# A wider opening, joined squares, a new task order and a later place for one gate in a two-layer decoder kernel

## The chip, the cores and the metric

The kernel runs on one core of a Trainium2 chip. Five engines of that core work side by side: TensorE (matmuls; the profile calls its matmuls PE and its weight loads PEld), VectorE (DVE), ScalarE (ACT), GpSimd (POOL) and SyncE (SP, which here only issues transfers). The metric is the device time of one execution in microseconds, as the median of several runs.

## The reference

Two layers run one after the other on 256 tokens of width 1024. Each layer has a token-mixing half and a retrieval half, and both are modulated by six vectors that come from the conditioning `c`:

```python
mod = (c_act @ w_ada + b_ada)[:, None, :]
sh1, sc1, g1, sh2, sc2, g2 = jnp.split(mod, 6, axis=-1)
h = rms_norm(x, norm1_g) * (1 + sc1) + sh1
proj = h @ w_in
q, k, v, cb, cc, ch, su, sv = jnp.split(proj, split_pts, axis=-1)
...
x = x + g1 * (merged @ w_out)
h2 = rms_norm(x, norm2_g) * (1 + sc2) + sh2
x = x + g2 * peer_ffn(h2, peer_wq, peer_sub_keys, peer_down, peer_up)
```

`merged` joins windowed attention with 8 query heads, a short gated convolution and a spatial gate over 128-token chunks, each with a norm of its own. `peer_ffn` projects `h2` to queries, scores them against two sets of 128 keys for each of 8 heads, picks 16 of 128 x 128 experts for each head, and adds their gated outputs. Note where the six vectors are used: `sh1`, `sc1` at the start of a layer, `g1` after the output projection, `sh2`, `sc2` right behind that, and `g2` only when the experts of the layer are done.

## The kernel before

**Layout.** The residual stream `X` lies in on-chip memory with the 1024 features as 8 chunks of 128 partitions and the 256 tokens along the free axis. A large buffer, `arena`, is cut by hand into regions whose use changes from stage to stage.

**Weights.** All weights come in as chunks of 128 x 1024 numbers (512 KB) from one list, `seq` (L352 to L377). `cast_step` takes the next entry of that list. A "mat" entry is split into a high half on ScalarE (L312, L314) and a low half on VectorE (L305, L307), both issued with raised priority (L310), and is used in three cheaper products (L401 to L403). A "whole" entry is used as it is, in one full-precision product (L399). Raw chunks lie in a ring of five buffers of two chunks each; a new transfer waits until both chunks of the oldest buffer have been used. `next_chunk` hands the next weight chunk to TensorE and keeps two more prepared.

**Modulation ("ada" entries).** The six vectors need 48 chunks of `w_ada` for each layer. VectorE multiplies each chunk by the activated `c` and sums along its free axis (L252), so one such entry costs a transfer of 512 KB and one VectorE pass, and no TensorE work. In layer 0 all 48 are spread among the other weights: groups sc1 and sh1 in the opening, g1, sh2 and sc2 among the input projection's chunks, g2 among the first six chunks of the output projection (`mix(tail[:6], ada(0, [5]))`, L363). `mix(a, b, first, last)` puts the entries of b evenly behind those of a between two positions.

**The opening of layer 0** (`first_norm` L454, `first_chunks` L555). The sum of squares is taken over 8 feature chunks: ScalarE squares each chunk (L457), TensorE sums each over its partitions by products with a column of ones (L440). Then follow the root, the reciprocal and a product that spreads the result over all partitions (L424). After that each of 8 row blocks d is taken in turn: two ada entries, a row block of the first `FIRST` input-projection chunks (`w_first[d]`, 128 x FIRST * 128 numbers, into `R_FIRST`), the scaled and shifted chunk d of the input (L450 on VectorE, L452 on ScalarE), and `FIRST` products with it (L559), accumulated in FIRST/2 PSUM banks. `FIRST` is 6, so two query pairs and the key/value pair are done in the opening.

**The rest of the input projection** (`mixing` L588). Chunks `FIRST` to 15 follow, one by one (`chunk`), each pair emptied by ScalarE (`evac`). Behind chunk n the tasks that `PLAN0` lists for n are issued: head sums (`qk_sums`), logits (`lg..`), softmax (`sm..`), transposes (`pt..`), value products (`pv..`), norms and so on. Numbers 16 to 23 stand between the chunks of the output projection. In this part the instructions' order on each engine is found by a list scheduler that follows program order as priority.

**The retrieval half** (`retrieval` L878). A hand-ordered bridge (`bridge` L468) computes the second norm beside the first query chunks; then chunks 4 to 15 of the query projection follow in pairs, with one group of score products for each pair (L995), while VectorE works off top-16 searches (L883 to L891) from a list of filling work. Then 128 expert chunks downwards (L399) and 128 upwards (L1214) run on TensorE, in a hand-written order. Picks become one-hot factors by three transposes for each half of the tokens (L977).

Of the kernel before, what the change touches and what calls it, by code (L numbers as in the profile page):

```python
# [13 lines left out]
AF = mybir.ActivationFunctionType  # L14
# [6 lines left out]
DC = 8  # L21
# [15 lines left out]
WHOLE_PQ = (0, 1)  # L37
WHOLE_OUT = ((4, 5), ())
OUT_ORDER = ((4, 5, 1, 0, 2, 6, 7, 3), (4, 5, 0, 3, 2, 1, 6, 7))
PLAN0 = ((5, 'qk_sums'), (7, 'k_norm lg01'), (8, 'exp sm01'), (9, 'v_tok lg00 sm00'), (10, 'lg10 lg11'), (11, 'pt01 pt00 cz'), (12, 'sm11 inv0 sm10 sg'), (13, 'pt10 pt11 pv0 inv1 ao0'), (14, 'cy as0 gs4 pv1 an0'), (15, 'gn4 mix'), (16, 'ao1 as1 sqrt'), (18, 'an1'), (19, 'gs6'), (20, 'gn6'))  # L40
PLAN1 = ((5, 'qk_sums k_norm'), (6, 'v_tok'), (7, 'lg10 exp'), (8, 'lg01 lg00 sm00'), (10, 'lg11'), (11, 'sm01 cz'), (12, 'sg'), (13, 'pt00 pt01 sm10 pv0'), (14, 'inv0 ao0 cy pt10'), (15, 'sm11 pt11 inv1 gs4 pv1 as0 ao1 gn4 mix'), (16, 'as1 an0'), (17, 'an1 sqrt'), (20, 'gs6 gn6'))
G_LAST = 124
OUT_AT = (3, 5, 6, 7)
# [21 lines left out]
FOLD_LAG = 4  # L65
FILL = 1.5
FILL_DOWN = (2.2, 2.1)
FIRST = 6
SUMS_AT = 5


# [12 lines left out]
def hybrid_trunk(ctx: ExitStack, tc: tile.TileContext, x_in, c_in, vec_in, w_ada, w_first, w_in, w_out, w_pq,  # L84
                 keys, down, down_rows, up, up_rows, rel_bias, sgu_w, sgu_b, out):
    nc = tc.nc
# [57 lines left out]
    X = region(56 * S, DC, S)  # L144
# [12 lines left out]
    R_YS = region(37 * S, DC, S)  # L157
# [45 lines left out]
    class Src:  # L203
# [6 lines left out]
        seq = []  # L210
# [125 lines left out]
    def ada(layer, groups, kind="ada"):  # L336
        return [(kind, w_ada[layer, p], (layer, p)) for g in groups for p in range(8 * g, 8 * g + 8)]
# [15 lines left out]
    for layer in range(DEPTH):  # L353
        body = [("whole" if n in WHOLE_IN[layer] else "mat", w_in[layer, n], None) for n in range(16)]
        tail = [("whole" if k in WHOLE_OUT[layer] else "mat", w_out[layer, k], vec[:, layer, V_OG + k:V_OG + k + 1])
                for k in OUT_ORDER[layer]]
        if layer == 0:
            first = []
            for d in range(DC):
                first += [("ada", w_ada[0, o + d], (0, o + d)) for o in (SC1, SH1)]  # L360
                first.append(("first", w_first[d], R_FIRST[:, d, :]))
            body = first + mix(body[FIRST:], ada(0, [2, 3, 4]))
        body += mix(tail[:6], ada(0, [5])) + tail[6:] if layer == 0 else tail  # L363
        seq += body + [("whole" if n in WHOLE_PQ else "mat", w_pq[layer, n], None) for n in range(16)]
        dn, un = ([("pair", None, None) if n % 2 else ("second" if n % 4 == 0 else "whole", w[layer, n // 2], None)
                   for n in range(128)] for w in (down, up))
        for n, at in enumerate(AHEAD_AT):
            c = AHEAD_FIRST + n
            dn[c] = ("early", down[layer, c // 2, :, c % 2, :], region(at * S, D))
        aside = ada(1, [0, 1, 2, 3, 4] if layer + 1 < DEPTH else [5], "aside")  # L370
        for n, at in reversed(tuple(enumerate(ASIDES_AT[layer]))):
            dn.insert(at, aside[n])
        if layer + 1 < DEPTH:
            un = mix(un, aside[len(ASIDES_AT[layer]):], *ASIDES_UP)
        Src.starts.append(len(seq))
        seq += dn + un
# [76 lines left out]

    def first_norm():  # L454
        ss = bank("g", 2)
        for d in range(DC):
            nc.scalar.activation(R_YS[:, d, :], X[:, d, :], AF.Square)  # L457
            sums(ss, d, d == DC - 1)
        rs = inv_rms(ss)

        def step(d):
            for _ in range(3):
                cast_step()
            scaled(R_HF[:, d, :], mods[0], SC1, SH1, rs, d)

        return step
# [1016 lines left out]
```

## Time and profile before

| | us |
|---|---|
| median of 3 runs | 1558.25 |
| lowest and highest run | 1555.5, 1559.74 |
| the profiled execution, whole time | 1555.62 |
| its span from first to last instruction | 1553.9 |
| opening, until the last product of the row blocks ends | 41.17 |
| first product of the output projection starts | 100.38 |
| first product of the bridge starts | 127.99 |
| score groups of the query projection, first and last | 148.53 to 186.90 |

The page gives busy time of each engine, busy tenths in 40 slices of the span, the transfer queues, and the chain of work that ended last, followed back from the last instruction. Views of the trace give the same for a chosen stretch. In a row of a group, "x32" counts instructions, then come busy time, the mean duration in ns, and the idle time before with what ended it. In a row of the timeline stand start, duration, engine, line, operation, result and operands; the bracket says how long the engine idled before it and what released it. One full-precision product appears as two records.

### The profile page before, as it was taken

What the parts mean: (1) busy time and instruction counts of PE and PEld (TensorE: products, weight loads), DVE (VectorE), ACT (ScalarE), POOL (GpSimd) and SP (SyncE); (2) the same over time, 40 slices, a digit from 0 to 9 for tenths busy, and PEclk for the clock granted to TensorE, in tenths of its full rate; (3) what the DMA queues carried; (4) which work ended last, traced back from release to release, by engine and by line L of the source; (5) the groups of instructions that cost most, each with busy time, mean ns of one, the idle gap of its engine ahead of it and who ended that gap; (6) DMA issues with size and microseconds to landing.
All of it is one profiled execution on the core that took longest, in us unless ns stands there. A gap on an engine that the chain in (4) does not pass through costs nothing.

```text
span 1553.9 us, 28477 instructions
## 1 busy us (share of the span) xinstructions
PE 1532.3 (99%) x11244; PEld 1494.4 (96%) x11244; DVE 1001.7 (64%) x2248; ACT 475.1 (31%) x1357; POOL 502.0 (32%) x424
## 2 busy tenths in 40 slices
PE   8999999999999999999999999999999999999998
PEld 7879999999999999999999899999999999999998
DVE  7787897577787454434457578976777764444434
ACT  2356312465564000000026663133666620000000
POOL 0000125333343434333400001244454445444441
PEclk9999999999999999999999999999999999999999
DMA  9998289999999999999975473899999999999996
GB/s 382 392 371 319 97 318 355 421 421 422 422 420 408 420 423 421 423 423 423 423 279 169 169 258 108 328 360 422 421 424 420 420 422 423 423 423 423 424 423 246
DMA packets 122119, 570.64 MB, mean 367 GB/s; under 512 B 14292, under 2 KB 14820, under 8 KB 89986
## 3 DMA queue, kind: packets, MB, share of 16 engines
q1 hardware_dynamic: 48818, 240.54, 39.1%
q0 software_dynamic: 55744, 202.36, 32.6%
q10 hardware_dynamic: 17424, 125.93, 19.6%
q8 instruction: 88, 1.44, 0.3%
q14 instruction: 45, 0.37, 0.1%
HBM read 563.50 MB, written 4.09 MB: 365 GB/s over the span
## 4 chain that ended last, share of the span: by engine, by line
PE 78%; DMA 8%; issue 6%; DVE 4%; POOL 3%; ACT 1%; SPq 0%; ACTq 0%; POOLq 0%; DVEq 0%
PE acc L1214 37%; PE ch L399 24%; DMA arena<-in_down_rows,arena 6%; PE ch L401 2%; PE ch L402 2%; PE ch L403 2%; POOL arena L1117 2%; DMA raw<-in_w_ada 2%; PE g L1176 1%; PE ch L490 1%; PE g L995 1%; PE acc L401 1%; DVE raw L252 1%; PE acc L403 1%; PE acc L402 1%
## 5 line engine op out<-in xcount | busy, mean ns | idle before, releaser
L1214 PE MATMUL acc<-arena,raw 128*128 128x168 f32 (+1 forms) x4096 | 572.7, 303 | 1.6 <-issue 1.6
L1214 PEld LDWEIGHTS acc<-arena,raw 128*128 128x128 f32 x4096 | 570.4, 190 | 2.4 <-issue 2.4
L399 PE MATMUL ch<-arena,raw 128*128 128x168 f32 (+2 forms) x3808 | 564.4, 307 | 1.9 <-issue 1.9
L399 PEld LDWEIGHTS ch<-arena,raw 128*128 128x128 f32 x3808 | 539.5, 190 | 8.7 <-issue 5.1
L1142 DVE SCALAR_TENSOR_TENSOR spots<-arena,spots 128x1024 f32<-128x1024 f32 x156 | 200.4, 1284 | 237.0 <-DMA arena<-in_up_rows,arena 236.3
L1117 POOL DMA_INDIRECT arena<-in_up_rows,arena x159 | 213.4, 1342 | 289.3 <-DMA arena<-in_up_rows,arena 198.0
L1117 POOL DMA_INDIRECT arena<-in_down_rows,arena x151 | 183.6, 1216 | 227.5 <-DVE arena L1127 167.9
L1127 DVE SCALAR_TENSOR_TENSOR arena<-arena,spots 128x1024 f32<-128x1024 f32 x151 | 183.0, 1223 | 65.6 <-DMA arena<-in_down_rows,arena 61.1
L1160 ACT ACTIVATE arena<-arena,parts 128x128 f16<-128x128 f16 x164 | 64.6, 394 | 128.6 <-DVE arena L1150 114.3
L430 ACT ACT_TABLE_LOAD x6 | 7.7, 1283 | 271.5 <-PE acc L1214 271.4
L401 PE MATMUL ch<-hh,hi 128*128 128x256 f32 x288 | 82.6, 288 | 2.0 <-DVE arena L521 1.9
L402 PE MATMUL ch<-hh,lo 128*128 128x256 f32 x288 | 81.8, 284 | 0.0
L403 PE MATMUL ch<-hh,hi 128*128 128x256 f32 x288 | 81.8, 284 | 0.0
L1193 ACT ACTIVATE arena<-ch 128x336 f32<-128x336 f32 (+32 forms) x122 | 42.2, 346 | 128.1 <-PE ch L399 103.3
L252 DVE SCALAR_TENSOR_TENSOR aside<-aside,arena 128x1024 f32<-128x1024 f32 x48 | 58.6, 1220 | 25.4 <-DMA aside<-in_w_ada 25.4
L252 DVE SCALAR_TENSOR_TENSOR raw<-raw,arena 128x1024 f32<-128x1024 f32 x48 | 58.7, 1228 | 13.2 <-DMA raw<-in_w_ada 9.2
L305 DVE TENSOR_TENSOR lo<-raw,hi 128x1024 fp32r<-128x1024 f32 x42 | 51.2, 1224 | 22.1 <-ACT hi L312 19.2
L399 PE MATMUL ch<-arena 128*128 128x168 f32 (+1 forms) x448 | 63.7, 303 | 1.7 <-issue 1.7
L1186 DVE SCALAR_TENSOR_TENSOR arena<-arena,g 128x336 f32<-128x336 f32 (+30 forms) x82 | 40.4, 492 | 37.9 <-ACT arena L1184 37.0
L399 PEld LDWEIGHTS ch<-arena 128*128 128x128 f32 x448 | 62.6, 190 | 2.2 <-issue 2.2
L1162 ACT ACTIVATE arena<-arena,parts 128x128 f16<-128x128 f16 x164 | 63.4, 386 | 0.0
L1164 ACT ACTIVATE arena<-arena,parts 128x128 f16<-128x128 f16 x164 | 63.4, 386 | 0.0
(237 smaller groups left out, 1722.7 us busy)
## 6 DMA issues: line engine op xcount, KB each, us to landing
raw<-in_up SPq DMA_DIRECT2D x64, 1024.0 KB
raw<-in_up ACTq DMA_DIRECT2D x64, 1024.0 KB
raw<-in_down SPq DMA_DIRECT2D x58, 1024.0 KB
raw<-in_down ACTq DMA_DIRECT2D x56, 1024.0 KB
raw<-in_w_ada SPq DMA_DIRECT2D x48, 512.0 KB
aside<-in_w_ada SPq DMA_DIRECT2D x48, 512.0 KB
raw<-in_w_pq SPq DMA_DIRECT2D x32, 512.0 KB
arena<-in_down SPq DMA_DIRECT2D x28, 512.0 KB
```

The costliest lines, as they stand in the source:

```text
L252: nc.vector.scalar_tensor_tensor(raw, raw, 1.0, cact, op0=OP.mult, op1=OP.mult, accum_out=mods[layer][:, col:col + 1])
L399: nc.tensor.matmul(dst, hi[:, cols], k[0], start=start, stop=stop, **kw)
L401: nc.tensor.matmul(dst, hi[:, cols], k[0], start=start, stop=False, **kw)
L402: nc.tensor.matmul(dst, lo[:, cols], k[0], start=False, stop=False, **kw)
L403: nc.tensor.matmul(dst, hi[:, cols], k[1], start=False, stop=stop, **kw)
L1117: nc.gpsimd.indirect_dma_start(out=held[n], out_offset=None, in_=rows if n >= TS else down_rows[:, :], in_offset=bass.IndirectOffsetOnAxis ...
L1127: nc.vector.scalar_tensor_tensor(row, row, 1.0, R_DX[which(k)[0]], op0=OP.mult, op1=OP.mult, accum_out=R_DOTS[:, k:k + 1])
L1142: nc.vector.scalar_tensor_tensor(R_SUM[s], row, w, R_SUM[s], op0=OP.mult, op1=OP.add)
L1160: nc.scalar.activation(og[0][:, 0, i, :], oh[:, 0, i, :], AF.Copy, scale=parts[:, 0, t + i:t + i + 1])
L1162: nc.scalar.activation(og[1][:, 0, i, :], oh[:, 0, i, :], AF.Copy, scale=parts[:, 1, t + i:t + i + 1])
L1164: nc.scalar.activation(og[0][:, 1, i, :], oh[:, 1, i, :], AF.Copy, scale=parts[:, 0, t + 2 + i:t + 3 + i])
L1214: nc.tensor.matmul(acc[d // 2][:, (d % 2) * S:(d % 2) * S + T], u[:, d * P:(d + 1) * P], acts[:, i, :], start=i == 0 and d % 2 == 0, stop= ...
```

## The change

It has five parts. Constants: `FIRST` is 8 instead of 6, so the opening computes eight chunks with four PSUM banks, `w_first` and `R_FIRST` grow by a third, and the chunks 6 and 7 are no longer in the ring. `PLAN0` gives the tasks of layer 0 another order. In `first_norm` each half of `X` (four feature chunks) is squared by one ScalarE instruction, VectorE adds the second pair of its squares to the first, and TensorE sums two joined chunks instead of four. The eight ada entries of g2 in layer 0 leave the output projection and stand behind chunks 6 to 13 of the query projection (`G2_AT`). Layer 1 has the code that it had.

```diff
-PLAN0 = ((5, 'qk_sums'), (7, 'k_norm lg01'), (8, 'exp sm01'), (9, 'v_tok lg00 sm00'), (10, 'lg10 lg11'), (11, 'pt01 pt00 cz'), (12, 'sm11 inv0 sm10 sg'), (13, 'pt10 pt11 pv0 inv1 ao0'), (14, 'cy as0 gs4 pv1 an0'), (15, 'gn4 mix'), (16, 'ao1 as1 sqrt'), (18, 'an1'), (19, 'gs6'), (20, 'gn6'))
+PLAN0 = ((7, 'qk_sums'), (8, 'k_norm'), (9, 'lg01 exp'), (10, 'sm01 v_tok lg00'), (11, 'sm00 lg10 lg11 cz'), (12, 'pt01 pt00 sm11 sg'), (13, 'inv0 sm10 pt10 pt11 pv0 inv1 ao0'), (14, 'cy as0 gs4 pv1 an0'), (15, 'gn4 mix'), (16, 'ao1 as1 sqrt'), (18, 'an1'), (19, 'gs6'), (20, 'gn6'))
...
-FIRST = 6
+FIRST = 8
+G2_AT = (5, 14)
...
-        body += mix(tail[:6], ada(0, [5])) + tail[6:] if layer == 0 else tail
-        seq += body + [("whole" if n in WHOLE_PQ else "mat", w_pq[layer, n], None) for n in range(16)]
+        queries = [("whole" if n in WHOLE_PQ else "mat", w_pq[layer, n], None) for n in range(16)]
+        seq += body + tail + (mix(queries, ada(0, [5]), *G2_AT) if layer == 0 else queries)
...
         ss = bank("g", 2)
-        for d in range(DC):
-            nc.scalar.activation(R_YS[:, d, :], X[:, d, :], AF.Square)
-            sums(ss, d, d == DC - 1)
+        for half in range(2):
+            at = 4 * half
+            nc.scalar.activation(R_YS[:, at:at + 4, :], X[:, at:at + 4, :], AF.Square)
+            nc.vector.tensor_add(R_YS[:, at:at + 2, :], R_YS[:, at:at + 2, :], R_YS[:, at + 2:at + 4, :])
+            for d in (at, at + 1):
+                sums(ss, d, d == 5)
```

## The prediction

> **What bounds the kernel now.** I read the page first: engines, slices, then the chain of work that ended last.
>
> ```profile
> PE 1532.3 (99%) x11244; PEld 1494.4 (96%) x11244; DVE 1001.7 (64%) x2248; ACT 475.1 (31%) x1357; POOL 502.0 (32%) x424
> PE   8999999999999999999999999999999999999998
> PE 78%; DMA 8%; issue 6%; DVE 4%; POOL 3%; ACT 1%; SPq 0%; ACTq 0%; POOLq 0%; DVEq 0%
> ```
>
> TensorE is busy from slice 2 to the end and carries the chain. So an edit is worth what it does to the time at which TensorE gets through the edited stages; what other engines save counts only where TensorE waits for them. Next, the table by stage (columns: stretch, its length, busy time of PE, PEld, DVE, ACT, POOL, clock, DMA share, GB/s): opening, input projection with attention, output projection, query projection.
>
> ```profile
> 0.00:41.00 41.00, 36.01 (x136) 29.13 (x137) 29.55 (x74) 12.43 (x27) 4.46 (x12) 1.00 0.97 384
> 41.00:100.00 59.00, 58.08 (x317) 47.03 (x315) 47.16 (x112) 25.89 (x72) 1.19 (x2) 1.00 0.98 384
> 100.00:128.00 28.00, 27.07 (x199) 26.16 (x200) 22.62 (x38) 11.54 (x19) 0.00 (x0) 1.00 0.95 372
> 150.00:185.00 35.00, 35.00 (x297) 35.00 (x296) 30.67 (x153) 14.60 (x21) 3.81 (x5) 1.00 0.29 103
> ```
>
> From 41 us on TensorE idles about 1 us in 59 and 1 us in 28, and the transfers run at 0.95 to 0.98 of their capacity up to 128 us. Only the query projection has transfers to spare (0.29). Both limits matter before 128 us, so I follow the chain through the opening.
>
> ```profile
> 13.57 9.06 DMA raw<-in_w_ada
> 22.70 8.86 DMA raw<-in_w_ada
> 31.58 1.24 DVE raw L252 x2
> ...
> 37.75 0.52 ACT arena L452
> 38.31 1.99 PE ch L559 x8
> 40.30 0.86 PE acc L559 x4
> 41.17 0.34 PE g L618 x4
> ```
>
> The opening is set by transfers, then by the last row block: chunk row on VectorE, bias on ScalarE, twelve matmul records (two per product) that end at 41.17. Behind it TensorE runs without a wait.
>
> **Part 1, joined squares.** The rows of the first norm, in time order:
>
> ```profile
> 6.16 6.99 PE L440 MATMUL g<-ones,arena 128*128 128x1 f32 x32
> 7.57 1.33 ACT L457 ACTIVATE arena<-arena 128x256 f32<-128x256 f32 x4 [0.59 <-DMA arena<-in_x_t]
> 8.95 1.22 DVE L252 SCALAR_TENSOR_TENSOR raw<-raw,arena 128x1024 f32<-128x1024 f32 x1 [4.00 <-ACT arena L457]
> 13.18 0.26 ACT L417 ACTIVATE rn<-g,eps 128x2 f32<-128x2 f32 x1 [2.98 <-PE g L440]
> 16.34 3.78 PE L559 MATMUL ch<-arena 128*128 128x256 f32 x8 [1.11 <-ACT arena L452]
> 154.30 1.05 ACT L312 CAST hi<-raw 128x1024 fp32r<-128x1024 f32 x1 [1.63 <-PE ch L403]
> 73.89 0.70 DVE L767 TENSOR_TENSOR arena<-arena 128x512 f32<-128x512 f32 x1
> ```
>
> Removed: six ScalarE squares and 16 of 32 sum records (6.99/32 = 0.218 us each, 3.5 us). Added: two VectorE adds. A square of 1024 columns is not in the trace; the nearest row of that width is 1.05 us, against 1.33 for the four it replaces (bounds 1.0 and 1.33). The add is 0.70. The second half now runs 7.57 + 1.05 + 0.70 + 8 x 0.218 = 11.1 us instead of 13.15, so the norm is about 2.1 us earlier and the first product starts near 14.2 instead of 16.34. If the second add queues behind the first ada chunk (8.95 to 10.17), only 0.9 us is left of that, because the sums wait behind it.
>
> **Part 2, eight chunks in the opening.** Sizes and the slow first products:
>
> ```profile
> raw<-in_w_ada SPq DMA_DIRECT2D x24, 512.0 KB
> arena<-in_w_first SPq DMA_DIRECT2D x8, 384.0 KB
> 19.91 1.91 PE L559 MATMUL acc<-arena 128*128 128x256 f32 x4
> 21.20 2.12 PEld L559 LDWEIGHTS ch<-arena 128*128 128x128 f32 x8
> 54.42 3.46 PE ch L399 x16
> ```
>
> Each row block grows from 384 to 512 KB. Seven of them lie before the last block's data: 7 x 131 KB = 0.92 MB, 2.2 us at about 420 GB/s. The last block starts at 38.31 + 2.2 = 40.5 and now has 16 records, 3.46 us (a whole chunk's row): end 44.0. TensorE's own path: the first 12 records took 16.34 to 21.20, 4.9 us, at half speed; after them 116 records at 3.46/16 = 0.216 make 25.1; 14.2 + 4.9 + 25.1 = 44.2 (45.4 if the second add is late). The two paths meet, so the joined squares are what keeps TensorE from setting the end. I take 44.1, which is 2.9 us later than 41.17. In return two chunks, 2 x 3.46 = 6.9 us, no longer run after it. Net gain 4.0 us, between 2.8 and 4.3.
>
> **Part 3, the projection behind it and the new task order.** Eight chunks are mixed with 24 ada chunks, three to one, instead of ten at 2.4 to one. Total bytes to the end of the stage are unchanged; they are only in another order.
>
> ```profile
> 48.46 1.66 DVE L252 SCALAR_TENSOR_TENSOR raw<-raw,arena 128x1024 f32<-128x1024 f32 x1 [4.56 <-DMA raw<-in_w_ada]
> arena<-in_rel_bias POOLq DMA_DIRECT2D x1, 1024.0 KB
> L252 DVE SCALAR_TENSOR_TENSOR raw<-raw,arena 128x1024 f32<-128x1024 f32 x24 | 29.6, 1236 | 5.8 <-DMA raw<-in_w_ada 5.8
> ```
>
> VectorE waits 4.56 us for a chunk while the bias table comes in on POOL's queue, so arrival sets the pace there. Afterwards one chunk and three ada chunks are 2 MB, 5.0 us per chunk, against 3.46 us of products plus tasks. By that pace the ninth chunk lands near 41, the tenth near 49 (the tables come between), then one each 5 us. TensorE ends the ninth at 47.6 and the head sums near 49.6, and has the key norm and first logits to fill the next gaps. I charge 0.6 us of new idle time (bounds 0, when tasks fill everything, and 2.5, half a chunk's pace, when the tasks wait on VectorE). The tasks are the same instructions in another order, and the fourth PSUM bank of the opening is emptied by ScalarE beside the ninth chunk's products, so neither adds a term.
>
> **Part 4, the last gate moves.** Eight ada chunks leave the output projection. There TensorE idles 0.93 us (28.00 - 27.07), so it can win 0 to 0.9; I take 0.3. They join the query projection, one behind each of chunks 6 to 13, with 512 KB each on SyncE's queue, where the 103 GB/s leave room. Rows that bound the cost:
>
> ```profile
> 156.73 1.21 DVE L305 TENSOR_TENSOR lo<-raw,hi 128x1024 fp32r<-128x1024 f32 x1
> 175.71 1.21 DVE L305 TENSOR_TENSOR lo<-raw,hi 128x1024 fp32r<-128x1024 f32 x1
> 157.14 0.89 PE g L995 x8
> 163.78 0.89 PE g L995 x8
> 177.08 0.89 PE g L995 x8
> 210.84 0.29 DVE L967 TENSOR_TENSOR arena<-arena 128x128 f32<-128x128 f32 x1
> 218.01 0.39 PEld L977 LDWEIGHTS g<-ident,arena 128*128 128x128 f32 x3
> ```
>
> Eight at 1.22 us are 9.8 us of VectorE; it has 35.00 - 30.67 = 4.3 us idle there, so it falls about 5.5 us behind. What TensorE needs of it is only the low half of each chunk. Between two score groups (157.14, 163.78) lie two chunks of (6.64 - 0.89)/2 = 2.9 us; the low half made by 157.9 is used from 160.9, the one made by 176.8 from 180.9: leads of 3 to 4 us. The low halves carry a raised priority, an ada chunk doesn't, so an ada chunk can delay one by at most its own 1.22 us. What falls behind is top-16 work. Its first product for TensorE is ready at 211.1 and used at 218.0: 6.9 us of cover for 5.5. I cost the move at 0; without the cover it is 5.5 to 9.8 us. Two queues see the move as well. On SyncE's the loads behind an ada chunk wait until its buffer pair is free; there are five pairs, so a load is asked for about three chunks (9 us) before its use, and 5.5 us of lag fit in. On ScalarE's own queue one expert load (L287) waits for such a pair with the casts behind it; it is issued four ring items late, about two chunks, which is more than the lag too.
>
> **Sum.** -4.0 + 0.6 - 0.3 + 0 = -3.7 us. Against the profiled execution (1555.62 us; span 1553.9) that is 1551.9. The median of the runs is 1558.25, 2.6 us above that execution; I forecast on the median: **1554.5 us**. About 0.3% (4.7 us) is what a measurement of this kernel can tell from no change, so the likeliest outcome is within it.
>
> **Rivals.**
> 1. *The idle time closes.* The two stages after the opening show 0.92 + 0.93 = 1.85 us of idle TensorE. If the new order and the relieved VectorE remove it, no new idle comes, and Part 2 gives its 4.3: 6.15 us, 1552.1. For it: the idle sits at the seam of attention and output projection, where VectorE was busy 22.62 of 28 us. Against: a wait there can be a dependence (norm, reciprocal, spread) rather than load.
> 2. *Arrival paces the projection.* DMA share 0.98 over 41 to 100 us: if TensorE waits for chunks 9 to 12, and VectorE's ada work delays the softmax, the 4.0 us are spent again: 1557.5 to 1558.5. Against: TensorE's work left in that stage, 58.08 - 6.9 = 51 us, is longer than the 40 us of eight arrivals.
> 3. *VectorE sets the query projection (slower).* If the order of VectorE's queue puts ada and top-16 work ahead of the low halves, TensorE loses 5.5 to 9.8 us between 150 and 185 us and the net is +1.8 to +6.1: 1560 to 1564.4. It decides once VectorE's lag passes the 3 to 4 us lead. For it: 5.5 exceeds the lead. Against: the raised priority.
> [...]
>
> **How the numbers follow.** Forecast 0.44; rival 1 0.20; rival 2 0.18; rival 3 0.13; rival 4 0.05. The runs shown before spread by 4.2 us (1555.5 to 1559.74), so a median may lie 2 us off. The range runs from rival 1 less that, rounded down, 1549.5, to the near end of rival 3, 1560; outside are most of rival 3 (0.12) and the tails of scatter, not over 0.08. Faster by over 0.3% needs more than 4.7 us: rival 1 (0.20), rival 4 without the stall (0.03), and the part of the forecast's own spread beyond 4.7 us (0.07): 0.30. Slower by over 0.3%: rival 3's upper part, 0.10. The rest, 0.60, is within.
>
> **What would show it.** Sums of the first norm at 16 records, ended near 11; the last opening product near 44 and the first output-projection product near 97 instead of 100.4; the first bridge product near 124 instead of 128; in the query projection score groups still 6.6 us apart and PE at 35 of 35; the first pick transposes without a wait before them. I am wrong if the opening ends past 45.5, if chunks of the projection wait on transfers for over 2 us in sum, or if the score groups spread.

## The result: slower by half a per cent, and where the time went

The changed kernel took 1567.63 us in the median of 11 runs (1563.1 to 1576.2), the kernel before 1560.79 us in 11 runs (1555.5 to 1562.8). The medians differ by 6.8 us; the ratio is 1.0051 with a 95% interval of 1.0036 to 1.0065, some 8 us. The forecast was 1554.5 and the range ended at 1560, so both missed, and the time moved the other way. The profiled execution of the changed kernel took 1566.4 us, its span is 1564.6. One trace below, that of the run sc2_in_output_old_order_g2_later, is of an execution of 1784.86 us at a clock of 0.832 and is not used.

First the page of the changed kernel: engines, PE slices and clock slices.

```profile
PE 1536.1 (98%) x11228; PEld 1497.2 (96%) x11228; DVE 1001.5 (64%) x2250; ACT 478.1 (31%) x1353; POOL 508.3 (32%) x424
PE   8989999999999999999999999999999999999998
PEclk9989999999999999999999999999999999999999
```

The third slice (78 to 117 us) is the only one early on in which PE and PEclk have both lost. The same stretches as in the prediction without the opening, for the changed kernel:

```profile
41.00:100.00 59.00, 53.99 (x280) 43.63 (x278) 45.75 (x108) 29.57 (x74) 3.04 (x5) 0.97 0.97 379
100.00:128.00 28.00, 26.43 (x178) 24.48 (x179) 14.13 (x24) 8.76 (x14) 0.00 (x0) 0.88 0.55 189
150.00:185.00 35.00, 34.83 (x294) 34.83 (x295) 33.33 (x124) 19.36 (x27) 2.62 (x3) 1.00 0.75 280
```

Between 41 and 100 us TensorE now idles 5.0 us where it idled 0.92, and its clock is no longer 1.00. The opening did about what it was charged for:

```profile
7.45 1.87 PE L441 MATMUL g<-ones,arena 128*128 128x1 f32 x8 [1.32 <-DVE arena L460]
10.05 1.87 PE L441 MATMUL g<-ones,arena 128*128 128x1 f32 x8 [0.74 <-DVE arena L460]
14.93 3.52 PE L563 MATMUL ch<-arena 128*128 128x256 f32 x8 [1.17 <-ACT arena L453]
42.93 1.89 PE L563 MATMUL acc<-arena 128*128 128x256 f32 x8
```

The sums have 16 records and end at 11.9, the second add (9.31) stood behind the first ada pass, and the last opening product ends at 44.82, 3.65 us later than 41.17. In return two chunks, 6.92 us, are gone from what follows. But the first output-projection product came at 105.21 instead of 100.38. So about 8.1 us (4.83 + 6.92 - 3.65) were lost between those two points. What TensorE waited for (engine, line, releaser, us, times, longest), first in the kernel before from 40 to 130 us, then in the changed kernel from 41 to 110 us:

```profile
PE g L424 <- DVE rg L418: 1.4, 2, 0.9
PE acc L399 <- DVE arena L718: 0.4, 1, 0.4
```

```profile
PE acc L679 <- ACT arena L669: 3.7, 2, 2.4
PE g L728 <- DVE ra L419: 1.4, 1, 1.4
PE g L425 <- DVE rg L419: 0.9, 1, 0.9
```

Not one wait is for a transfer. The transposes (L679) wait for the exponentials (L669), 3.7 us in all; two norms wait for their reciprocals (L419), 2.3 us. The timeline shows what is behind the longest wait of each kind:

```profile
83.59 1.19 DVE L253 SCALAR_TENSOR_TENSOR raw<-raw,arena 128x1024 f32<-128x1024 f32 x1
84.71 0.88 DVE L776 SCALAR_TENSOR_TENSOR arena<-arena,vec 128x256 f32<-128x256 f32 x2
85.50 0.16 DVE L666 TENSOR_SCALAR m<-m 128x4 f32<-128x4 f32 x1
85.70 0.51 ACT L669 ACTIVATE arena<-arena,m 128x256 f32<-128x256 f32 x1 [2.13 <-DVE m L666]
86.35 1.18 PE L679 MATMUL acc<-ident,arena 128*128 128x128 f32 x4 [2.39 <-ACT arena L669]
87.33 4.80 PE L400 MATMUL ch<-arena,raw 128*128 128x256 f32 x16
...
99.03 1.28 DVE L308 SCALAR_TENSOR_TENSOR lo<-raw,vec,hi 128x1024 fp32r<-128x1024 f32 x1 [0.36 <-ACT hi L315]
100.23 0.16 DVE L419 RECIPROCAL ra<-ra 128x1 f32<-128x1 f32 x1
```

VectorE works through an ada pass (L253) and a convolution step; only then comes the tiny softmax step (L666, 0.16 us), then ScalarE, then TensorE. And the chunk behind it takes 4.80 us, where a chunk of the kernel before takes 3.62 in the same view. The second kind is another: at 99.03 VectorE makes a low half of an output-projection chunk (L308), and the norm's reciprocal stands behind it. Windows of 1 us in the changed kernel (the last three columns are clock, DMA share, GB/s) say why the chunk is slow:

```profile
85.00:86.00 1.00, 0.00 (x0) 0.00 (x0) 1.00 (x7) 0.30 (x1) 0.00 (x0) 1.00 1.04 426
87.00:88.00 1.00, 1.00 (x5) 0.91 (x5) 1.00 (x2) 1.00 (x6) 0.00 (x0) 0.50 1.03 410
...
101.00:102.00 1.00, 0.24 (x2) 0.00 (x0) 1.00 (x2) 0.89 (x1) 0.00 (x0) 0.50 0.95 352
```

The clock is at half (0.50) from about 86.3 to 89.7, behind a gap of 2.4 us, and from about 100 to 106.8 us, where gaps of 1.4 and 0.9 us lie (99.05 and 101.24); a gap of 1.3 us at 75.85 left it at 1.00. Between opening and output projection idle time grew from 1.30 to 6.36 us, by about 5; the other 3 of the 8.1 are put down to the work at half clock there, some 7 us of it (an estimate: at 0.50 that work would lose up to 3.5 us). The sums of the engines by 10 us, first the kernel before, then the changed one, show that the load on VectorE is not new:

```profile
70.00:80.00 10.00, 9.94 (x54) 8.40 (x53) 10.00 (x29) 7.42 (x31) 0.00 (x0) 1.00 1.02 400
80.00:90.00 10.00, 10.00 (x55) 7.31 (x54) 9.27 (x28) 9.20 (x23) 0.00 (x0) 1.00 1.03 418
```

```profile
70.00:80.00 10.00, 8.49 (x41) 6.83 (x40) 10.00 (x26) 5.83 (x22) 0.00 (x0) 1.00 0.98 350
80.00:90.00 10.00, 7.44 (x29) 5.29 (x29) 10.00 (x33) 6.34 (x22) 0.00 (x0) 0.83 1.03 417
```

VectorE was full, or nearly so, in both. Before, TensorE was full as well, and the two hid each other. The change took 6.9 us from TensorE alone.

Further on: the output projection itself neither won nor lost much (first product to first update 25.49 us before, 25.90 after), and about 1.3 us were lost in the bridge (below), so that the score groups of the query projection are 6.6 us late. The rest up to 10.7 us of span comes and goes in the experts and in layer 1, whose code is the same.

### The profile page after: what moved, and what is told of

Read it like the earlier page. It is cut to its first block, busy times and chain, and to the rows that moved or that the text cites. A ratio compares the mean times of both kernels' runs of the same rounds, so it can differ in the third digit from the quotient of the medians.

```text
span 1564.6 us, 28450 instructions
## 1 busy us (share of the span) xinstructions
PE 1536.1 (98%) x11228; PEld 1497.2 (96%) x11228; DVE 1001.5 (64%) x2250; ACT 478.1 (31%) x1353; POOL 508.3 (32%) x424
## 3 DMA queue, kind: packets, MB, share of 16 engines
q0 software_dynamic: 55744, 202.36, 32.4%
## 4 chain that ended last, share of the span: by engine, by line
PE 72%; DMA 15%; DVE 5%; issue 4%; ACT 2%; POOL 2%; SPq 0%; ACTq 0%; DVEq 0%; POOLq 0%
PE acc L1218 36%; PE ch L400 20%; DMA arena<-in_down_rows,arena 10%; DMA raw<-in_w_ada 3%; PE ch L402 2%; PE ch L403 2%; PE ch L404 2%; POOL arena L1121 2%; PE g L1180 1%; DVE raw L253 1%; DMA raw<-in_down 1%; PE g L999 1%; PE ch L494 1%; DVE arena L1131 1%; PE acc L402 1%
## 5 line engine op out<-in xcount | busy, mean ns | idle before, releaser
L1121 POOL DMA_INDIRECT arena<-in_up_rows,arena x159 | 216.6, 1363 | 286.4 <-DMA arena<-in_up_rows,arena 212.3
L1164 ACT ACTIVATE arena<-arena,parts 128x128 f16<-128x128 f16 x164 | 64.6, 394 | 126.8 <-DVE arena L1154 126.8
L253 DVE SCALAR_TENSOR_TENSOR raw<-raw,arena 128x1024 f32<-128x1024 f32 x48 | 58.5, 1224 | 13.4 <-DMA raw<-in_w_ada 12.5
L253 DVE SCALAR_TENSOR_TENSOR aside<-aside,arena 128x1024 f32<-128x1024 f32 x48 | 58.5, 1219 | 7.6 <-DMA aside<-in_w_ada 7.6
L1166 ACT ACTIVATE arena<-arena,parts 128x128 f16<-128x128 f16 x164 | 63.4, 386 | 0.0
L1168 ACT ACTIVATE arena<-arena,parts 128x128 f16<-128x128 f16 x164 | 63.4, 386 | 0.0
L1170 ACT ACTIVATE arena<-arena,parts 128x128 f16<-128x128 f16 x164 | 63.3, 386 | 0.0
```

Of the source, the lines that this page charges most:

```text
L253: nc.vector.scalar_tensor_tensor(raw, raw, 1.0, cact, op0=OP.mult, op1=OP.mult, accum_out=mods[layer][:, col:col + 1])
L1121: nc.gpsimd.indirect_dma_start(out=held[n], out_offset=None, in_=rows if n >= TS else down_rows[:, :], in_offset=bass.IndirectOffsetOnAxis ...
L1164: nc.scalar.activation(og[0][:, 0, i, :], oh[:, 0, i, :], AF.Copy, scale=parts[:, 0, t + i:t + i + 1])
L1166: nc.scalar.activation(og[1][:, 0, i, :], oh[:, 0, i, :], AF.Copy, scale=parts[:, 1, t + i:t + i + 1])
L1168: nc.scalar.activation(og[0][:, 1, i, :], oh[:, 1, i, :], AF.Copy, scale=parts[:, 0, t + 2 + i:t + 3 + i])
```

## Experiments

The theory after the result: **VectorE's ada passes set the end of the attention**; chunks taken from TensorE become waits and then half clock, and the moved gate is a second, smaller cost. Rivals: the new task order, the moved gate alone, the squares, the arrival of transfers. All kernels ran beside the kernel before, but in four rounds on three chips, in which the median of before was 1559.65 to 1563.41; so ratios are to be compared, not medians. The table has what the sections need: ratio to before, then from one profiled execution each the start of the first output-projection product, of the first bridge product, and the distance from the first residual update (before: 125.87) to the third group of eight score products (before: 156.98). All are read in the timeline, where the first bridge product of before stands at 127.83.

| kernel | median, us | ratio (95%) | first output product | first bridge product | update to scores |
|---|---|---|---|---|---|
| before | | 1 | 100.38 | 127.83 | 31.11 |
| changed | 1567.63 | 1.0051 (1.0036 to 1.0065) | 105.21 | 133.07 | 32.45 |
| squares_alone | 1561.72 | 1.0006 (0.9990 to 1.0022) | 98.27 | 129.94 | 31.11 |
| opening_alone | 1566.08 | 1.0040 (1.0024 to 1.0056) | 105.94 | 134.47 | 31.11 |
| g2_late_alone | 1565.91 | 1.0024 (1.0005 to 1.0043) | 102.42 | 130.64 | 32.50 |
| g2_put_back | 1569.14 | 1.0049 (1.0031 to 1.0067) | 103.82 | 131.53 | 31.10 |
| old_order | 1571.61 | 1.0068 (1.0045 to 1.0090) | 103.71 | 132.09 | 32.41 |
| sc2_short_pass | 1572.55 | 1.0059 (1.0039 to 1.0080) | 106.71 | 134.92 | 32.69 |
| all_short_passes | 1554.98 | 0.9973 (0.9959 to 0.9987) | 97.98 | 123.80 | 32.69 |
| before_all_short | 1558.42 | 0.9995 (0.9981 to 1.0009) | 96.61 | 126.65 | 31.09 |

### Which part of the change costs

The parts one by one: the squares in the kernel before; the eight-chunk opening with them; the g2 entries moved in the kernel before; the changed kernel with one part undone.

```diff
 squares_alone: before, with the new first_norm
 opening_alone: before, with the new first_norm and
-FIRST = 6
+FIRST = 8
 g2_late_alone: before, with
+        seq += body + tail + (mix(queries, ada(0, [5]), *G2_AT) if layer == 0 else queries)
 g2_put_back: changed, with
+        body += mix(tail[:6], ada(0, [5])) + tail[6:] if layer == 0 else tail
 old_order: changed, with
+PLAN0 = ((5, 'qk_sums'), (7, 'k_norm lg01'), (8, 'exp sm01'), ...
```

> The kernel before with the joined squares alone. The opening of the kernel before is set by transfers, so the norm comes 1.4 us earlier, the last opening product is within 0.5 us of 41.17, and the time is within 1 us of before. Rival (the squares moved something that costs): 2 us or more slower.

> The wider opening and the joined squares alone: the changed kernel with the task order of before and g2 back in the output projection. Theory: VectorE's load sets the end, so most of the loss is there without the new order and without the move: first output-projection product at 101.5 to 104, first bridge product at 129.5 to 132, 3 to 7 us slower than before. Rival (the loss is made by the new order or the move): first output-projection product at 100.5 or earlier, not slower than before.

> The kernel before with the last part of the change alone: the eight g2 entries stand in the query projection. Theory (VectorE sets the end of the attention; the moved entries are a small second cost): the first output-projection product stays near 100.4, the output projection gains 0 to 0.9 us, and the entries that VectorE takes up inside the bridge cost about 1.3 us there, so 0 to +1.3 us in all, near 1561 to 1562 beside a before of 1560.8. Rival (the moved entries are the main cost): +5 us or more, with the first score group more than 5 us later than 157.1.

> The changed kernel with the eight g2 entries back among the first six chunks of the output projection. Theory (VectorE sets the end of the attention): the first output-projection product stays near 105, the bridge gets its 1.3 us back, the output projection takes back 0 to 0.9 us: 0 to 1.3 us less than the changed kernel, still 6 us or more slower than before. Rival (the moved entries are the main cost): within 2 us of before.

> The changed kernel with the task order of the kernel before: head sums, key norm, first logits and the exponentials stand ahead of chunks 8 and 9. Theory (VectorE is full from 60 to 92 us whatever the order): attention starts at most 2 us earlier, since the bias table and the passes are where they were; the first output-projection product is at 103 to 105. Rival (the new order is the cause): the first logits come 4 us or more earlier than 58.0 and the first output-projection product is at 100 or earlier, with 5 us or more won.

The squares alone cannot be told from no change, as expected. Yet in that trace the bridge starts 2.1 us later than in the kernel before (129.94 against 127.83), behind a wait of 1.9 us for VectorE in the output projection: a landmark can move by 2 us for no part of the opening. The opening alone is as much slower as expected, though its landmarks lie 2 us later than that (105.94 and 134.47); the old order is where it was expected (103.71), with first logits at 57.91, as early as in the changed kernel (58.01). The opening with the squares costs 0.40%, the moved gate alone 0.24%, and both together under the old order 0.68%, near their sum; the new order seems to take back some of it (1.0051 against 1.0068, but the intervals overlap). So the rival that the order makes the loss falls, and the moved gate alone is dearer than expected: 3.7 us by the ratio (0.8 to 6.7), of which 1.3 were foreseen after the result. Putting it back in the changed kernel gave back 1.4 us at each of two places in the profile and nothing in the time (1.0049 against 1.0051), within what was expected; that the move adds to the time of the changed kernel is thus not shown. Both places can be seen. In the bridge of the changed kernel:

```profile
144.41 1.22 DVE L253 SCALAR_TENSOR_TENSOR raw<-raw,arena 128x1024 f32<-128x1024 f32 x1 [0.41 <-DMA raw<-in_w_ada]
145.56 0.48 DVE L535 SCALAR_TENSOR_TENSOR hh<-arena,mod,hh 128x256 fp32r<-128x256 f32 x1
146.10 0.39 PE L404 MATMUL acc<-hh,hi 128*128 128x256 f32 x1 [1.06 <-DVE hh L535]
```

One g2 pass stands between the low halves of the tokens (L535), with 0.41 us of waiting for its own chunk, and TensorE stands 1.06 us behind. The last column of the table carries this through: every kernel with the gate moved has 32.4 to 32.7, every one without it 31.1. In front of the output projection it is an indirect effect. With no g2 entries in between, the transfers of that projection's weight chunks are issued earlier (all eight by 92.96 us in the changed kernel, by 107.44 in the kernel before), and the first low half of them is made earlier (at 101.23 in the kernel before, at 97.89 in the run with the gate moved alone). In that run:

```profile
97.89 1.28 DVE L308 SCALAR_TENSOR_TENSOR lo<-raw,vec,hi 128x1024 fp32r<-128x1024 f32 x1
99.09 0.16 DVE L419 RECIPROCAL rg<-rg 128x2 f32<-128x2 f32 x1
99.39 1.19 PE L425 MATMUL g<-ident,rg 128*128 128x128 f32 x4 [2.17 <-DVE rg L419]
```

The norm's reciprocal waits behind a low half that is not needed yet (the first product with a low half starts at 113.05), TensorE waits 2.17 us, and half clock follows (0.50 from 98 to 104 us). In the kernel before this wait is 0.85 us and the clock stays at 1.00. That the low half is the cause is read from this order, not tried by itself. The waits of 1.4 and 0.9 us in the changed kernel (99.03 above) are of this kind. With the gate put back there is one of 1.2 us in their place, with an ada pass among the work ahead of the reciprocal.

### Is it VectorE?

```diff
 sc2_short_pass, all_short_passes, before_all_short (first: SC2 <= col < SC2 + 8)
+        n = 16 if layer == 0 and G1 <= col < G2 else D
-        nc.vector.scalar_tensor_tensor(raw, raw, 1.0, cact, op0=OP.mult, op1=OP.mult,
+        nc.vector.scalar_tensor_tensor(raw[:, :n], raw[:, :n], 1.0, cact[:, :n], op0=OP.mult, op1=OP.mult,
```

> The changed kernel with the eight sc2 passes on VectorE cut to 16 of their 1024 columns; their transfers stay. It leaves out most of the sums of sc2. Theory (VectorE's passes delay the softmax): about 8 x 1.1 = 9 us less work on VectorE before the attention ends, so the exponentials come 4 to 9 us earlier, TensorE keeps its full clock between 80 and 110 us, and the first output-projection product is at 97 to 100 instead of 105.2; time near or below before. Rival (arrival of the chunks paces the projection): transfers are the same, so the first output-projection product stays within 1.5 us of 105.

> The changed kernel with all 24 passes of g1, sh2 and sc2 on VectorE cut to 16 of 1024 columns; their transfers stay. It leaves out most of the sums of these three vectors. Theory (VectorE's full queue between 59 and 92 us delays the softmax and also holds the buffers, so that the transfers pause): the transfers no longer pause near 68 us, the last softmax reciprocal comes 8 us or more before 90.0, and the first output-projection product is at 93 to 98, paced by arrival alone (44.8 us plus 17 MB at about 420 GB/s is 85 us for the last chunk, then the rest of the attention). Rival (arrival alone sets it, also in the changed kernel): the first output-projection product stays within 1.5 us of 105.

> The kernel before with the same 24 passes of g1, sh2 and sc2 cut to 16 of 1024 columns as in the changed kernel's run; it leaves out most of the sums of these three vectors. Theory (the wider opening's gain is real and only VectorE's load hid it): with VectorE out of the way the kernel before is the slower of the two: first output-projection product 3 to 5 us later than 97.98, first bridge product at 126 to 129 instead of 123.8, time within 2 us of before. Rival (the relief alone made the fast run, and the wider opening is worth nothing even then): first bridge product at 124.5 or earlier, time 4 us or more below before.

Eight short passes missed: the last softmax reciprocal came 4.3 us earlier (85.66 instead of 89.96), but the product came later, not earlier. In that run's order the last input chunk stands behind the first value products:

```profile
88.60 1.98 PE L693 MATMUL acc<-arena 128*64 128x512 f32 x4 [1.45 <-ACT arena L683]
90.51 1.81 PE L401 MATMUL ch<-arena,raw 128*128 128x256 f32 x4
```

The order of every engine is planned before the run, and with shorter passes it is another; that this lost what was won on VectorE is read from the order, not tried. Twenty-four short passes hit. The changed kernel with them, then the kernel before with them (60 to 100 and 100 to 128 us):

```profile
60.00:100.00 40.00, 39.55 (x215) 30.70 (x215) 22.21 (x97) 23.59 (x64) 0.56 (x1) 1.00 0.93 355
100.00:128.00 28.00, 28.00 (x202) 26.87 (x201) 17.61 (x30) 14.98 (x27) 0.55 (x1) 1.00 0.70 257
```

```profile
60.00:100.00 40.00, 39.23 (x224) 32.50 (x224) 20.62 (x84) 20.11 (x61) 0.56 (x1) 1.00 0.99 382
100.00:128.00 28.00, 26.40 (x191) 25.41 (x190) 21.88 (x37) 13.87 (x23) 0.00 (x0) 0.94 0.91 347
```

In the changed kernel TensorE is full and at full clock again, both kinds of waits are gone, and the first bridge product is at 123.80, where the prediction had put it (near 124). The relief takes the changed kernel from 1.0051 to 0.9973, some 12 us, and the kernel before only to 0.9995, under 1 us. That is the evidence for the theory: what costs time in the changed kernel is VectorE's load. (Short passes also free their chunks' buffers earlier and come with another order of instructions; these effects were not separated from it.) With it out of the way the change is ahead by 0.22% (3.4 us) in the ratios, whose intervals just overlap, and by 2.85 us at the bridge (123.80 and 126.65). How much of this lead is the wider opening's is not shown. The kernel before with short passes has a stall of its own in the output projection:

```profile
106.85 0.84 PE L425 MATMUL g<-ident,rg 128*128 128x128 f32 x4 [1.17 <-DVE rg L419]
```

The g2 passes, left at full length and standing there because this kernel does not move the gate, are taken to delay the norm; VectorE is busy 21.88 of 28 us there, but no view shows its order in that stretch. With another wait of 0.4 us, and a clock that is estimated at half from about 107.3 to 110.7 us (a product takes 0.41 us instead of 0.28, the mean clock is 0.94 from 100 to 128 us; some 1.5 us lost), this costs about 3 us, as much as the whole lead at the bridge. So the nearness to the 3.7 of the forecast proves nothing. Two expectations failed in part. The first output product of before came at 96.61, earlier and not later; chunks and attention are interleaved otherwise there (a sum of the attention, L712, still runs at 100.17), so the bridge is the better mark. And the transfers still pause near 67 us with short passes (85 and 55 GB/s between 66.5 and 69.5 us, beside over 400 before), so that pause is not made by VectorE's passes.

### Can the load be moved or reordered?

Three ways on the changed kernel: raised priority for logits and softmax; the sc2 entries moved to the output projection; half of the passes multiplied on GpSimd and summed on ScalarE.

```diff
 softmax_first
+                if layer == 0 and name[:2] in ("lg", "sm"):
+                    with tc.high_priority(offset=AHEAD):
+                        tasks[name]()
 sc2_in_output (with the old PLAN0: sc2_in_output_old_order; and G2_AT = (9, 16): ..._g2_later)
+            body = first + mix(body[FIRST:], ada(0, [2, 3]))
+        body += mix(tail[:6], ada(0, [4])) + tail[6:] if layer == 0 else tail
 half_moved (with g2 back, and then the old PLAN0; and on before: before_half_moved)
+        if layer == 0 and G1 <= col < G2 and col % 2:
+            nc.gpsimd.tensor_mul(raw, raw, cact)
+            nc.scalar.activation(raw, raw, AF.Copy, accum_out=mods[layer][:, col:col + 1])
```

> The changed kernel with raised priority for the logits and the softmax, so that these go ahead of the passes on VectorE; nothing else changes. Theory (passes ahead of softmax steps, and buffers held by passes that wait): the last softmax reciprocal comes 2 to 5 us earlier than 90.0, but the passes then hold the buffers longer, the last input chunk comes later, and the first output-projection product gains at most 2 us (103 to 106). Rival (only the order on VectorE's queue matters): first output-projection product at 100 or earlier.

> The changed kernel with the eight sc2 entries, transfers and passes, moved from the input projection into the first six chunks of the output projection, where VectorE is busy 14 of 28 us and the transfers take 0.55. Theory (VectorE and, through its buffers, the transfers are too full before 92 us): the last softmax reciprocal comes 4 us earlier as in the run with short sc2 passes, and the last input chunk comes earlier as well because 4 MB less are ahead of it, so the first output-projection product is at 97 to 100 and the time is 5 to 8 us below the changed kernel, between -1 and +3 us against before. Rival (the lost time is TensorE's clock or scatter, not this load): first output-projection product at 103 or later.

> The run with the sc2 entries in the output projection, with the task order of before. In that run chunk products went first and the first logits came only at 62.6; the old order starts them ahead of the next chunks. Theory: 9.8 us less on VectorE before 92 us and attention started early give a first output-projection product at 97.5 to 100.5, first bridge product at 124 to 127; less the bridge's 1.3 us for g2, 0 to 3 us below before. Rival: transfers pause when chunks wait for tasks, first output-projection product at 102 or later, slower than before.

> The run before this one with the g2 entries behind chunks 9 to 15 of the query projection instead of 6 to 13. Theory (the moved entries that VectorE takes up inside the bridge cost about 1.3 us there): the first score group comes 0.8 to 1.5 us earlier against the first bridge product than in the run before this one. Rival (the cost was not theirs): the same distance within 0.4 us.

> The changed kernel, but every second one of the 24 passes of g1, sh2 and sc2 is taken from VectorE: GpSimd multiplies and ScalarE sums. Theory (VectorE's load before 92 us sets the end of the attention): 12 x 1.22 = 14.6 us less on VectorE, the last softmax reciprocal near 82 to 86 and the first output-projection product at 98 to 101 instead of 105.2; 4 to 6 us less than the changed kernel, within 2 us of before. Rivals: GpSimd's multiplication is so slow, or slows VectorE's passes so much, that nothing is won (product at 104 or later); or the lost time is not VectorE's at all (the same).

> The same with the eight g2 entries back in the output projection. Theory: with them gone (as in the run that moved them alone) the output projection's weight halves, which have raised priority, go ahead of the last norms on VectorE, and its first product came 2 us later; with them back this goes, and the bridge's 1.3 us too: first output-projection product 1 to 2 us earlier than in the run before this one, first bridge product near 124 to 126, and 3 to 5 us below the kernel before. Rival: the g2 entries cost the output projection as much as they cost elsewhere: within 1 us of the run before this one.

> The same as the run with the g2 entries back, with the task order of the kernel before. Theory: with VectorE relieved the order that starts the attention earlier is at least as good: first output-projection product within 1 us of the run before this one, or up to 2 us earlier. Rival: the new order is what the eight-chunk opening needs: 2 us or more later, as TensorE waits for exponentials.

> The kernel before, with the same 12 passes taken from VectorE and nothing of the change. Theory: in the kernel before TensorE waits little before 100 us (0.92 of 59 us), so relief of VectorE alone is worth at most 1 us there: first output-projection product at 99 to 100.4, time within 2 us of before, and 2 to 4 us slower than the eight-chunk opening with the same relief. Rival: the relief is worth as much here, and the wider opening nothing: within 1 us of the eight-chunk runs with relief.

| kernel | median, us | ratio (95%) | first output product | last softmax reciprocal |
|---|---|---|---|---|
| softmax_first | 1567.87 | 1.0058 (1.0038 to 1.0078) | 105.72 | 90.17 |
| sc2_in_output | 1563.44 | 1.0039 (1.0022 to 1.0056) | 104.68 | 93.93 |
| sc2_in_output_old_order | 1569.16 | 1.0060 (1.0041 to 1.0079) | 106.98 | 91.52 |
| half_moved | 1570.10 | 1.0056 (1.0037 to 1.0076) | 108.58 | 90.91 |
| half_moved_g2_back | 1568.69 | 1.0044 (1.0026 to 1.0062) | 106.56 | 91.05 |
| half_moved_g2_back_old_order | 1561.85 | 1.0008 (0.9991 to 1.0025) | 102.29 | 85.94 |
| before_half_moved | 1560.78 | 1.0003 (0.9986 to 1.0019) | 100.16 | 78.14 |

None is faster than the kernel before. Of what was expected, softmax_first's first product came (105.72), half_moved_g2_back's gain of 2 us at that product, and before_half_moved's product and time; the rest did not. The raised priority left VectorE's order from 59 to 92 us as it was, so this run is a second reading of the changed kernel and no test of the rival. With sc2 moved the first product came at 104.68, which is where the rival had it (103 or later); the last softmax step was not earlier but 4 us later. The timeline of that run:

```profile
88.80 1.21 DVE L253 SCALAR_TENSOR_TENSOR raw<-raw,arena 128x1024 f32<-128x1024 f32 x1
89.93 1.28 DVE L308 SCALAR_TENSOR_TENSOR lo<-raw,vec,hi 128x1024 fp32r<-128x1024 f32 x1
...
93.32 0.69 DVE L708 TENSOR_TENSOR arena<-acc,arena 128x512 f32<-128x512 f32 x1 [0.89 <-PE acc L693]
93.93 0.17 DVE L674 RECIPROCAL m<-m 128x4 f32<-128x4 f32 x1
```

Passes and low halves still run ahead of the last softmax step, and that step then stands behind a sum (L708) which waits for TensorE. So these entries, moved, did not relieve VectorE in time, and the run neither confirms the theory nor excludes its rival. With the old order it was no better, against the expectation. The run with g2 still later gave 1.0063 (1.0044 to 1.0082); without a usable trace, what the bridge would do with later entries stays open.

GpSimd failed by the rival that was named for it. Groups of VectorE and of GpSimd from 41 to 100 us, then two rows of the timeline:

```profile
L257 DVE SCALAR_TENSOR_TENSOR raw<-raw,arena 128x1024 f32<-128x1024 f32 x12 | 21.8, 1822 | 3.4 <-DMA raw<-in_w_ada 3.4
...
L254 POOL TENSOR_TENSOR raw<-raw,arena 128x1024 f32<-128x1024 f32 x12 | 30.0, 2510 | 21.0 <-DMA raw<-in_w_ada 15.2 <-DVE raw L257 2.9 <-PE g L643 1.4
...
68.36 2.37 POOL L254 TENSOR_TENSOR raw<-raw,arena 128x1024 f32<-128x1024 f32 x1 [1.34 <-DVE st L754]
69.00 2.80 DVE L257 SCALAR_TENSOR_TENSOR raw<-raw,arena 128x1024 f32<-128x1024 f32 x1
```

Twelve passes instead of 24, but each takes 1822 ns instead of 1232. The one that starts at 69.00 under GpSimd's product (68.36 to 70.73) takes 2.80 us, of which only the last 1.07 lie behind that product. Those at 76.24 and 79.92, with no product of GpSimd beside them, take 1.21. An operation on 128 x 8 numbers (L272) took 1.99 us from 65.04, beside GpSimd's product from 64.66 to 67.01, and 0.17 us at 100.11, with no such product beside it. In two of the other three kernels with half the passes moved the mean pass takes 1895 and 2052 ns, and in the third (half_moved_g2_back) one pass takes 2.80 us (at 69.04), so VectorE was not free in any of them. The last two rows of the table are what the rival of before_half_moved had named (no gain from the wider opening, under 1 us apart by their ratios); as VectorE was loaded in both, they do not decide.

## Why the prediction was wrong, step by step

**The bound.** "TensorE carries the chain" was right for the kernel before, but the prediction took it for the only bound. The table by stage showed VectorE at 47.16 of 59 us, 80%, and was not cut finer. By 10 us it is 10.00, 10.00 and 9.27 between 60 and 90 us. None of the prediction's three signs of being wrong appeared; none of them looked at VectorE ahead of the output projection.

**Part 1** held in its second form: the second add behind the first ada pass, the sums ended at 11.9. The first product came at 14.93, 1.4 us earlier; the text had 2.1, or 0.9 with that add behind (by its own rows, 10.17 + 0.70 + 8 x 0.218, the sums would then end only 0.5 us earlier). Alone it is worth nothing measurable: in squares_alone the opening, which transfers set, ends at 40.96 instead of 41.17.

**Part 2** was mis-sized by 0.7 us: the opening ends at 44.8, not 44.1, so the net is 3.3 instead of 4.0. Its bounds of 2.8 and 4.3 come out of its own times as 2.7 and 4.1.

**Part 3 is the step that failed.** It charged 0.6 us of idle time with bounds of 0 and 2.5; the profile shows about 8.1 us lost, 5 of them idle. Its sentence that the tasks "are the same instructions in another order", so "neither adds a term", counted instructions on TensorE and not VectorE's queue behind which they wait: 24 passes of 1.23 us and the attention fill it from 59 to 92 us in either kernel (32.3 and 32.8 of 33 us), and the last softmax reciprocal moved from 86.26 to 89.96 instead of forward. The bound of 2.5 was taken from the arrival of chunks; no wait of TensorE on a transfer appeared. And no term stood for the clock: it went to half around the gaps (0.50 in the windows above), which cost about 3 us more by the estimate given there. With the passes cut short the bridge starts where the sum had put it; that the rest of the sum is right is likely, but the stall in its counterpart leaves it open.

**Part 4** missed in size at both ends. The output projection did not win 0.3 us (it took 0.4 longer, its first 1.6 us still at half clock, to about 106.8), and the move cost 1.3 us in the bridge, a stage that the part did not price. The query projection itself went as written: groups 6.6 us apart, and no wait of TensorE for a low half. The pick transposes did not wait (first at 224.73, 6.6 us later than 218.15, as all before it). A rule in that part, that an ada pass can delay a low half by at most its own 1.22 us, held nearly: one pass with 0.41 us of its own wait in front.

**Rivals.** The first one hoped for idle time to close; it grew. The second one named the mechanism ("VectorE's ada work delays the softmax") and gave it 0.18, but priced it at the 4.0 us of the opening, 1557.5 to 1558.5. Its counter-argument compared TensorE's 51 us with the 40 us of eight arrivals, two quantities of which neither was the bound. The third put the loss by VectorE into the query projection, where it did not come. The fourth, which has 0.05, is about a stall of ScalarE in the kernel before, beside which TensorE loses 1.00 + 0.69 = 1.7 us:

```profile
229.12 0.45 ACT L1193 ACTIVATE arena<-ch 128x336 f32<-128x336 f32 x1 [9.49 <-remote]
226.00:228.00 2.00, 1.00 (x6) 0.78 (x5) 1.70 (x14) 0.00 (x0) 1.69 (x3) 1.00 0.93 324
228.00:230.00 2.00, 1.31 (x9) 0.98 (x8) 1.13 (x10) 0.45 (x1) 1.00 (x2) 1.00 0.97 377
```

It did not show as a loss: the stall is absent at that place in the changed kernel, where TensorE is busy 2.00 of 2 us in both windows. What made it, no run shows.

**The base.** The profiled execution of before, 1555.62 us beside a median of 1560.79, had a mean clock of 0.999; the 92 runs of before beside the later kernels have 0.990 to 0.997. So it was a lucky draw. Layer 1 shows it; windows of 780 to 830 us, of before and of squares_alone, whose code there is the same:

```profile
780.00:830.00 50.00, 49.91 (x367) 48.76 (x366) 29.76 (x47) 20.22 (x42) 0.00 (x0) 1.00 0.66 244
```

```profile
780.00:830.00 50.00, 49.46 (x322) 47.64 (x321) 29.21 (x47) 18.60 (x39) 0.92 (x2) 0.90 0.63 236
```

So the part of the 10.7 us that arose after 193 us (about 4) is not put down to the change. What exactly makes it up was not settled. The forecast also stood on a median of 3 runs, 1558.25; with 11 it is 1560.79, so 2.5 us of the 13.1 between forecast and result lie in the base.

## What to carry to other kernels

Where two engines are full side by side, as TensorE (9.94 and 10.00 of 10 us) and VectorE (10.00 and 9.27) were here from 70 to 90 us, work taken from one can turn into waiting on the other: before counting what leaves the bound engine, cut its neighbours' load into windows as short as the gain. Cut the suspected work to almost nothing in both kernels, the old and the new, since only the pair tells whether the gain is hidden or absent; and look in both traces for stalls that have nothing to do with the question. A pass that nobody waits for still costs when it stands in front of a small step that everybody waits for: here one of 1.19 us (at 83.59) ahead of a step of 0.16 us (at 85.50), with TensorE waiting 2.39 us.

## What the hardware showed that was not expected

**The clock fell after short gaps.** In the changed kernel it fell to 0.50 at the end of 2.4 us without products (to 86.35), but stayed at 1.00 over 1.3 us (to 77.19). In g2_late_alone it fell less than 1 us after TensorE stopped at 97.2, soon after a series of products with a single column (95.05 to 96.75). In layer 1 of the changed kernel it fell with TensorE busy throughout:

```profile
808.00:810.00 2.00, 2.00 (x21) 2.00 (x19) 1.08 (x3) 1.35 (x5) 0.00 (x0) 0.98 0.49 96
811.00:814.00 3.00, 3.00 (x11) 2.63 (x11) 1.94 (x6) 2.12 (x6) 0.00 (x0) 0.50 0.37 150
```

The low stretches lasted about 3.4 us (86.3 to 89.7) or about 6.8 us (100.0 to 106.8 and 809.9 to 816.8 in the changed kernel, 97.9 to 104.7 in g2_late_alone); these are estimates from the clock in windows of 1 us (for the first 0.66, 0.50, 0.50 and 0.64). In old_order a gap lasted 3.8 us (to 78.09), and there the clock fell only at about 79, with products running again, as estimated from its mean of 0.98 over 60 to 80 us. Where it fell less than 1 us into a gap, or with none, narrow products ran just before (1 or 64 columns); whether that is the reason was not tested.

**GpSimd's product held VectorE up.** In half_moved, beside 2.35 us of GpSimd (from 64.66), an operation of VectorE that takes 0.17 us at 100.11 lasted 1.99 us (from 65.04), so an idle GpSimd was no spare engine for this work.
